# Scaling the attention's latents and shared rotary key on POOL during the input projection, with a round trip through DRAM, in place of DVE at the attention's entry

## The chip, the core and the metric

The kernel runs on one core of a Trainium2 chip. The metric is the device time of one execution in microseconds (us). A core has five engines with queues of their own, each worked off in order: PE (TensorE, matrix products), DVE (VectorE), ACT (ScalarE), POOL (GpSimd) and SP, which here only issues transfers. Sixteen DMA engines move the data. Engines wait for each other through semaphores.

## The reference, cut to what matters

One layer of an encoder on 1024 tokens of width 1024, all in float32. One input projection feeds a convolution branch, a retention branch, a latent attention and a gate; the branches are gated, joined and projected, and the input is added.

```
h = rmsnorm(x, norm_g);  u = h @ w_in            # conv GLU 2*512 | retention q,k,v 3*512 |
                                                 # q-latent 384 | kv-latent 256 | rope key 64 | gate 2048
q  = rmsnorm(q_lat, qa_g)  @ w_uq                # 8 heads x (128 + 64 rotary)
kv = rmsnorm(kv_lat, kva_g) @ w_ukv              # 8 heads x (128 key + 128 value)
k_rope = apply_rope(u_kr, cos, sin)              # one key for all heads
p = softmax((q_nope k_nope + q_rope k_rope) * 192 ** -0.5);  o = p @ v
y = concat(conv, retention, o) * silu(u_gate);   out = rmsnorm(x + y @ w_out, final_g)
```

rmsnorm of a latent is a product of every column (token) with one number, the inverse root of its mean square, and of every row with a weight. The number per token is what the change moves.

## The kernel before, in words

Everything lies transposed: channels on the 128 partitions, tokens along the row. A product in float32 is made of three products of rounded parts (`mm3`, lines 172 to 175): each operand is split into a high part (ACT, a cast) and a low part (DVE, `split_l`, line 66, recorded as line 61).

The input projection is 21 units of 256 columns (`run_unit`), each of four groups of 24 products into one PSUM bank; `run_v` is its form for retention values. Units 0 to 3 make the convolution, 4 to 7 gates, 8 to 10 the latents and the rotary key (`ev_lat`): each half, 128 x 512, is multiplied with the row `rbc`, stored to `l_dram` and squared for the latent's norm. `row_rsqrt` turns the squares into the inverse roots, which go to `lq_dram` and `lk_dram`. Units 11 to 13 make keys, queries and values of the retention, 14 a gate, 15 to 17 the other two heads of the retention, 18 to 20 gates. A retention unit leaves its bank by three DVE products with a table (`ev_rope`, lines 433 to 435); for units 15 and 16 the tables are the two tiles b, loaded at lines 421 and 422 and multiplied with `rbc` on POOL (`trig`). From unit 15 on the projection has only two banks for its groups (`MAIN2`).

Work beside the projection is written as generators in the list `bg`, from which `tick` takes a few steps behind each group: `conv_gen` and `conv_post` (the convolution and its end, with four loads of gates in eight halves, line 373), later `ret_gen` (the retention of one head). Behind unit 14 `drain` empties the list, the pool `cv` on the right side of SBUF is closed, and the pool `rt` of the retention takes its place. Its first tiles are b, the decay index (w, lines 494 and 496), the decay tables Dm, kd and qd made from it, and the pieces w.

The order of the instructions of each engine is not that of the program: the compiler's scheduler lays them out by a simulated timeline, and tiles that reuse memory wait for the last reader of what lay there. Once laid out, each engine's order is fixed.

At the attention's entry (lines 663 to 701) the latents come back: `lat(i, h)` loads half h of latent i from `l_dram`, multiplies it with the broadcast row (`rows`, DVE, line 680), and splits it with the weight into lH (ACT, 681) and lL (DVE). `lat_rows` loads the rows. The rotary key's halves kr are loaded and multiplied with a table (DVE, line 698). The entry's products are `g_k`, `g_r`, `g_kr`, `g_q`, `g_v`; `g_r2` turns the rotary part of q, with four small DMAs and three POOL operations, and Unit.qk (lines 811 to 815) makes the scores.

Of the kernel before, what the change touches and what calls it, by code (L numbers as in the profile page):

```python
# [8 lines left out]
F32 = mybir.dt.float32  # L9
# [4 lines left out]
ADD, SUB, MUL, MAX = ALU.add, ALU.subtract, ALU.mult, ALU.max  # L14

P = 128
S = 1024
D = 1024
KT = D // P
HS = 512  # L20
# [7 lines left out]
QT = 3  # L28
KVT = 2
NG = 16  # L30
EPS = 1e-6
# [23 lines left out]
def body(tc, xT, x, w_in, w_uqn, w_uqr, w_uk, w_uv, w_out, vecs, decay, final_g,  # L55
         t_ret, t_mla, t_idx, t_iota, idm, out):
    nc = tc.nc
    act, dve, pool, pe, sp = nc.scalar, nc.vector, nc.gpsimd, nc.tensor, nc.sync
# [4 lines left out]
    def tt(eng, o, a, b, op):  # L63
        eng.tensor_tensor(o, a, b, op=op)

    def split_l(eng, lo, src, hi, scale=1.0):
        stt(eng, lo, src, scale, hi.bitcast(F32), MUL, SUB)
# [20 lines left out]
    def ps_bg():  # L88
        rr["b"] += 1
        return ps(BG[rr["b"] % len(BG)])  # L90

    def mk(pl, shape, dt=F32, tag=None, bufs=None):
        cnt[0] += 1
        kw = {} if bufs is None else {"bufs": bufs}
        return pl.tile(shape, dt, name=f"{tag}{cnt[0]}", tag=tag, **kw)
# [2 lines left out]
    g_dram = [tc.dram_tile([P, S], F32, name=f"g_dram{i}") for i in range(NG)]  # L98
    y_dram = [tc.dram_tile([P, S], F32, name=f"y_dram{i}") for i in range(NG)]
    l_dram = [tc.dram_tile([P, S], F32, name=f"l_dram{i}") for i in range(QT + KVT + 1)]  # L100

    vec = mk(const, [P, NV], tag="vec")
    rcol = mk(const, [P, KT], tag="rcol")
# [20 lines left out]
    cv = cvx.enter_context(tc.tile_pool(name="cv", bufs=1, side="right"))  # L124
# [90 lines left out]
    bg = []  # L215
# [48 lines left out]
    for k in range(KT):  # L264
# [8 lines left out]
        n = S // 4 if XN[k] == 4 else HS  # L273
# [19 lines left out]
    def row_rsqrt(ss, scale, eps, o, d, col=None):  # L293
        if col is None:
            col = mk(const, [P, KT], tag="rrc", bufs=2)
        c = ps_bg()
        for n in range(KT):
            pe.matmul(c[:, n:n + 1], ss[:, n * P:(n + 1) * P], ones[:, 0:1], start=True, stop=True)  # L298
        dve.tensor_scalar(col, c[:, :KT], scale, eps, op0=MUL, op1=ADD)
        pool.tensor_tensor(col, col, eps_c[:, :KT], op=ALU.pow)  # L300
        pe.transpose(c[:KT, P:2 * P], col, ident)
        row = mk(cv, [P, HS], tag="cb", bufs=2)[:KT, :P]
        act.copy(row, c[:KT, P:2 * P])
        sp.dma_start(d.rearrange("(n p) -> n p", p=P), row)
        if o is not None:
            sp.dma_start(o, d.rearrange("(o s) -> o s", o=1).to_broadcast([P, S]))
# [85 lines left out]
    lss = mk(cv, [P, S], tag="lss")  # L392
    lsk = mk(cv, [P, S], tag="lsk")
# [19 lines left out]
        wn = run_unit(u, wn, ev_lat(2 * (u - 8)), u + 1, 2)  # L413
    lq_dram = tc.dram_tile([S], F32, name="lq_dram")
    lk_dram = tc.dram_tile([S], F32, name="lk_dram")
    for ss, n, d in ((lss, 384.0, lq_dram), (lsk, 256.0, lk_dram)):
        row_rsqrt(ss, 1.0 / n, EPS, None, d)

    def trig(pl, tag):
        c, s_ = mk(pl, [P, S], tag=tag, bufs=2), mk(pl, [P, S], tag=tag, bufs=2)  # L420
# [212 lines left out]
    fin, la, wt, lx = late  # L633
# [26 lines left out]
    def half(i):  # L660
        return slice(i * HS, (i + 1) * HS)

    def row_bc(pl, tag, d, h):
        t = mk(pl, [P, HS], tag=tag)
        sp.dma_start(t, d[half(h)].rearrange("(o s) -> o s", o=1).to_broadcast([P, HS]))
        return t

    krt, rows = [], {}

    def lat_rows(h):  # L670
        rows[1, h] = row_bc(fin, "rb", lk_dram, h)
        rows[0, h] = row_bc(wt, "xh", lq_dram, h)

    def lat(i, h):
        pl, tag, n = LT.pop(0)
        LT.append((pl, tag, n))
        t = mk(pl, [P, HS], tag=tag, bufs=n)
        sp.dma_start(t, l_dram[i][:, half(h)])
        g = vec[:, V_QG + i:V_QG + i + 1]
        tt(dve, t, t, rows[int(i >= QT), h], MUL)  # L680
        act.activation(lH[i][:, half(h)], t, AF.Identity, scale=g)
        split_l(dve, lL[i][:, half(h)], t, lH[i][:, half(h)], g)

    LT = [(lx, "lt", LTB)] * LTB + [(fin, "osb", 2), (fin, "g", 2)] * 2
    lat_rows(0)
    lat(3, 0)
    lat(4, 0)
    W = {("k", 0): lw_k(0)}
    for i in range(QT):
        lat(i, 0)  # L690
# [1 line left out]
    W["q", 0] = lw_q(0)  # L692
    W["v", 0] = lw_v(0)
    for h in range(2):
        t, tk = mk(lx, [P, HS], tag="kr", bufs=2), mk(fin, [P, HS], tag="g" if h else "osb", bufs=2)
        sp.dma_start(t, l_dram[5][:, half(h)])
        sp.dma_start(tk, t_mla[2][:, half(h)])
        tt(dve, t, t, tk, MUL)
        krt.append(t)
    sp.dma_start(cosm, t_mla[0])  # L700
    sp.dma_start(sinm, t_mla[1])
# [51 lines left out]
    def g_r(p, hf):  # L753
        o = up3(W["r", p], 0, QT, hf)
        xr = mk(wt, [P, HS], tag="xr")
        xs = mk(wt, [P, HS], tag="xs")
        act.copy(xr, o)
        for q in range(4):
            s0 = (q ^ 1) * 32
            sp.dma_start(xs[q * 32:(q + 1) * 32], xr[s0:s0 + 32])  # L760
        rst[p, hf] = xr, xs
# [100 lines left out]

    g_k(0, 0)
    g_r(0, 0)
    lat_rows(1)
    lat(3, 1)
    lat(4, 1)
    g_kr()
# [43 lines left out]
    for u in range(NUN):  # L912
# [33 lines left out]
        for i in range(8):  # L946
            cur.qk(i)
            t, j = (i // 2 - 1) % 4, i % 2
# [203 lines left out]
```

## Time and profile before

| what | value |
|---|---|
| median of 3 runs | 1118.09 us (1115.96 to 1120.15) |
| profiled execution, its own time | 1115.07 us |
| span of its trace | 1113.3 us |
| granted PE clock, mean | 0.996 |
| PE busy | 1095.2 us (98%), 5568 instructions |
| DVE / ACT / POOL busy | 724.1 (65%) / 412.6 (37%) / 149.8 us (13%) |

The profile is one execution. "Busy" is time in which the engine had an instruction in work; products of PE overlap, so their durations are longer than the distance from one to the next. The granted clock is the share of full speed (2.4 GHz) that PE's throttle gave. A transfer's "landing" is the time from its issue to its completion.

### The profile page before, as it was taken

How to read it: one execution, taken by the hardware profiler on the slowest of the kernel's cores; microseconds unless marked ns; L12 is line 12 of the kernel's file. 1: busy time of each engine (PE TensorE's matmuls, PEld its weight loads, DVE VectorE, ACT ScalarE, POOL GpSimd, SP SyncE). 2: the span in 40 equal slices, each digit the busy share in tenths (PEclk: the TensorE clock that was granted, in tenths of full speed). 3: DMA queues.
4: the chain of work that ended last, by engine and by line, in shares of the span. 5: the costliest groups of instructions: out<-in, count | busy, mean ns of one | idle time of the engine just before them, and what ended most of it. 6: DMA issues, size and time to landing. Idle time of an engine off the chain costs nothing.

```text
span 1113.3 us, 14293 instructions
## 1 busy us (share of the span) xinstructions
PE 1095.2 (98%) x5568; PEld 919.4 (83%) x5568; DVE 724.1 (65%) x1011; ACT 412.6 (37%) x741; POOL 149.8 (13%) x134
## 2 busy tenths in 40 slices
PE   9999999999999999999899999999999999999997
PEld 7888888888898899888678888888788877888886
DVE  7599999999747695746865565655565572535033
ACT  8211221122144134224654554544554462424022
POOL 0200000214302442020201101100110000001000
PEclk9999999999999999999999999999999999999999
DMA  7221223221262122227211111211210141835013
GB/s 272 95 58 66 86 92 126 85 86 48 97 216 94 49 76 66 96 76 248 79 39 47 56 35 49 62 35 45 63 44 30 57 143 38 308 98 203 25 45 107
DMA packets 45620, 101.33 MB, mean 91 GB/s; under 512 B 5616, under 2 KB 9568, under 8 KB 45552
## 3 DMA queue, kind: packets, MB, share of 16 engines
q1 hardware_dynamic: 45504, 100.35, 27.3%
q8 instruction: 43, 0.70, 0.3%
q14 instruction: 25, 0.20, 0.1%
q0 software_dynamic: 48, 0.08, 0.0%
HBM read 74.14 MB, written 24.17 MB: 88 GB/s over the span
## 4 chain that ended last, share of the span: by engine, by line
PE 93%; DVE 2%; ACT 1%; DMA 1%; issue 1%; SPq 0%; POOLq 0%; POOL 0%; DVEq 0%; ACTq 0%
PE ps L173 24%; PE ps L174 24%; PE ps L175 24%; PE ps L829 5%; PE ps L811 3%; PE ps L815 3%; PE ps L814 3%; PE ps L813 3%; PE ps L812 3%; PE ps L574 1%; PE ps L563 1%; PE ps L298 1%; PE ps L578 1%; PE ps L576 1%; DMA hp<-in_xT_dram 1%
## 5 line engine op out<-in xcount | busy, mean ns | idle before, releaser
L174 PE MATMUL ps<-xL,wh 128*128 128x512 f32 (+1 forms) x612 | 238.1, 390 | 0.1
L175 PE MATMUL ps<-xH,wl 128*128 128x512 f32 (+1 forms) x612 | 237.9, 389 | 0.0
L173 PE MATMUL ps<-xH,wh 128*128 128x512 f32 (+1 forms) x612 | 235.7, 392 | 2.0 <-ACT xH L137 1.5
L61 DVE SCALAR_TENSOR_TENSOR acc<-hp,cwh,acc 128x1024 f32<-128x1024 f32 x120 | 153.0, 1316 | 0.1
L173 PEld LDWEIGHTS ps<-xH,wh 128*128 128x128 f32 x612 | 114.7, 188 | 25.6 <-ACT xH L137 1.7
L174 PEld LDWEIGHTS ps<-xL,wh 128*128 128x128 f32 x612 | 115.0, 188 | 23.8 <-DVE xL L61 0.6
L175 PEld LDWEIGHTS ps<-xH,wl 128*128 128x128 f32 x612 | 114.9, 188 | 23.7 <-issue 0.2
L61 DVE SCALAR_TENSOR_TENSOR PL<-ps,PH 128x512 fp32r<-128x512 f32 x128 | 85.5, 684 | 54.5 <-ACT PH L831 54.3
L831 ACT CAST PH<-ps 128x512 fp32r<-128x512 f32 x128 | 72.8, 588 | 92.6 <-PE ps L829 92.0
L174 PE MATMUL ps<-woL,yh 128*128 128x512 f32 (+1 forms) x264 | 100.9, 386 | 0.0
L175 PE MATMUL ps<-woH,yl 128*128 128x512 f32 (+1 forms) x264 | 100.2, 386 | 0.0
L173 PE MATMUL ps<-woH,yh 128*128 128x512 f32 (+1 forms) x264 | 100.1, 386 | 0.0
L818 DVE TENSOR_REDUCE nm<-ps 128x1 f32<-128x1024 f32 x64 | 78.1, 1220 | 31.8 <-PE ps L815 31.1
L164 ACT CAST wh<-wraw 128x1024 fp32r<-128x1024 f32 x40 | 42.1, 1053 | 126.6 <-PE ps L174 117.0
L820 ACT ACTIVATE P<-ps,nm 128x1024 f32<-128x1024 f32 x64 | 71.6, 1119 | 26.1 <-DVE nm L818 23.7
L829 PE MATMUL ps<-ident,P 128*128 128x128 f32 x512 | 72.7, 273 | 0.0
L829 PEld LDWEIGHTS ps<-ident,P 128*128 128x128 f32 x512 | 61.5, 140 | 12.7 <-DVE PL L61 0.7
L61 DVE SCALAR_TENSOR_TENSOR wl<-wraw,wh 128x1024 fp32r<-128x1024 f32 (+2 forms) x45 | 54.3, 1207 | 7.4 <-ACT wh L164 6.3
L811 PE MATMUL ps<-kH,qH 128*128 128x512 f32 x128 | 55.0, 430 | 3.8 <-DVE qL L61 2.6
L174 PEld LDWEIGHTS ps<-woL,yh 128*128 128x128 f32 x264 | 49.6, 188 | 10.4
L173 PEld LDWEIGHTS ps<-woH,yh 128*128 128x128 f32 x264 | 49.6, 188 | 10.4
L175 PEld LDWEIGHTS ps<-woH,yl 128*128 128x128 f32 x264 | 49.6, 188 | 10.3
(291 smaller groups left out, 1987.0 us busy)
## 6 DMA issues: line engine op xcount, KB each, us to landing
wraw<-in_w_in_dram SPq DMA_DIRECT2D x40, 512.0 KB, 3.5
wor<-in_w_out_dram SPq DMA_DIRECT2D x16, 512.0 KB, 5.0
g_dram<-ga SPq DMA_DIRECT2D x29, 256.0 KB, 2.1
yr<-y_dram SPq DMA_DIRECT2D x18, 256.0 KB, 3.7
g<-g_dram SPq DMA_DIRECT2D x16, 256.0 KB, 3.3
rb<-rs_dram SPq DMA_DIRECT2D x16, 256.0 KB, 3.2
y_dram<-osb SPq DMA_DIRECT2D x16, 256.0 KB
z<-in_x_dram SPq DMA_DIRECT2D x8, 512.0 KB, 3.4
```

Of the source, the lines that this page charges most:

```text
L61: eng.scalar_tensor_tensor(o, a, s, b, op0=op0, op1=op1)
L164: act.copy(hi, t)
L173: pe.matmul(o, sh, mh, start=first, stop=False, skip_group_check=skip)
L174: pe.matmul(o, sh, ml, start=False, stop=False, skip_group_check=skip)
L175: pe.matmul(o, sl, mh, start=False, stop=last, skip_group_check=skip)
L811: pe.matmul(o, qh[:, ts], kh, start=True, stop=False)
L812: pe.matmul(o, qh[:, ts], kl, start=False, stop=False)
L813: pe.matmul(o, ql[:, ts], kh, start=False, stop=False)
L818: dve.tensor_reduce(nm, self.S, axis=AX.X, op=MAX, negate=True)
L820: act.activation(p, self.S, AF.Exp, bias=nm, accum_out=self.rs[:, t:t + 1])
L829: pe.transpose(o[:, c * P:(c + 1) * P], self.p[t][:, (4 * j + c) * P:(4 * j + c + 1) * P], ident)
L831: act.copy(ph, o)
```

## The change

The inverse roots of both latents are also kept as broadcast rows in the pool `cv` (`row_rsqrt` with a target tile, one more 512 KB load each). A new generator, `lat_gen`, goes to the end of `bg`: for each of the twelve halves of five latents and the rotary key it loads the half from `l_dram` into a tile "cb" (two of these, shared with the loads of `conv_post`), multiplies it on POOL with its row, or the rotary key with its table, and stores it to the new tensor `n_dram`. At the entry `lat` loads from `n_dram` and only splits; the row loads, the table loads and twelve DVE products are gone there.

```
     lq_dram = tc.dram_tile([S], F32, name="lq_dram")
     lk_dram = tc.dram_tile([S], F32, name="lk_dram")
-    for ss, n, d in ((lss, 384.0, lq_dram), (lsk, 256.0, lk_dram)):
-        row_rsqrt(ss, 1.0 / n, EPS, None, d)
+    rows = []
+    for ss, n, d, tag in ((lss, 384.0, lq_dram, "lss"), (lsk, 256.0, lk_dram, "lsk")):
+        rows.append(mk(cv, [P, S], tag=tag))
+        row_rsqrt(ss, 1.0 / n, EPS, rows[-1], d)
+
+    def lat_gen():
+        for i in (3, 4, 0, 1, 2, 5):
+            for h in range(2):
+                t = mk(cv, [P, HS], tag="cb", bufs=2)
+                hs = slice(h * HS, (h + 1) * HS)
+                sp.dma_start(t, l_dram[i][:, hs])
+                yield
+                if i < 5:
+                    tt(pool, t, t, rows[int(i >= QT)][:, hs], MUL)
+                else:
+                    k = mk(cv, [P, HS], tag="ca", bufs=4)
+                    sp.dma_start(k, t_mla[2][:, hs])
+                    tt(pool, t, t, k, MUL)
+                sp.dma_start(n_dram[i][:, hs], t)
+                yield
+
+    bg.append(lat_gen())
...
-        sp.dma_start(t, l_dram[i][:, half(h)])
+        sp.dma_start(t, n_dram[i][:, half(h)])
         g = vec[:, V_QG + i:V_QG + i + 1]
-        tt(dve, t, t, rows[int(i >= QT), h], MUL)
         act.activation(lH[i][:, half(h)], t, AF.Identity, scale=g)
         split_l(dve, lL[i][:, half(h)], t, lH[i][:, half(h)], g)
...
-        t, tk = mk(lx, [P, HS], tag="kr", bufs=2), mk(fin, [P, HS], tag="g" if h else "osb", bufs=2)
-        sp.dma_start(t, l_dram[5][:, half(h)])
-        sp.dma_start(tk, t_mla[2][:, half(h)])
-        tt(dve, t, t, tk, MUL)
+        t = mk(lx, [P, HS], tag="kr", bufs=2)
+        sp.dma_start(t, n_dram[5][:, half(h)])
```

The two calls of `lat_rows` and `row_bc` are gone as well. In the changed kernel the lines move: `lat_gen`'s load is line 427 and its store 435, the tables b are loaded at 442 and 443, the decay index at 515 and 517, the bank's evictions stand at 454 to 456.

The scheduler's order changes with it. On SP, at the end of unit 14, the loads of the tables b stood right behind the convolution's last store (y_dram) and the weights (wraw):

```order
L375 DMA y_dram_83<-acc_369 128x1024
L163 DMA wraw_2714<-in_w_in_dram 128x1024
L421 DMA b_2601<-in_t_ret_dram 128x1024
L422 DMA b_2602<-in_t_ret_dram 128x1024
L494 DMA w_2607<-in_t_idx_dram 128x256
L496 DMA w_2609<-in_t_iota_dram 128x256
L212 DMA g_dram_72<-ga_2499 128x512
L212 DMA g_dram_72<-ga_2529 128x512
```

In the changed kernel the same loads on SP stand behind all twelve loads (cb from l_dram) and stores (n_dram) of `lat_gen`, of which these are the last:

```order
L435 DMA n_dram_103<-cb_2542 128x512
L427 DMA cb_2550<-l_dram_98 128x512
L435 DMA n_dram_104<-cb_2546 128x512
L427 DMA cb_2584<-l_dram_101 128x512
L435 DMA n_dram_104<-cb_2550 128x512
L427 DMA cb_2590<-l_dram_101 128x512
L435 DMA n_dram_107<-cb_2584 128x512
L435 DMA n_dram_107<-cb_2590 128x512
L442 DMA b_2663<-in_t_ret_dram 128x1024
L443 DMA b_2664<-in_t_ret_dram 128x1024
L515 DMA w_2669<-in_t_idx_dram 128x256
L517 DMA w_2671<-in_t_iota_dram 128x256
```

The four gate stores (g_dram), which stood behind the tables, now stand between the loads and stores of `lat_gen`.

On PE, in unit 15, the first products of the retention (w with w) stood inside the unit's second group (ps_2724):

```order
L174 MATMUL ps_2724<-xL_122,wh_2487 128x512
L175 MATMUL ps_2724<-xH_114,wl_2488 128x512
L173 MATMUL ps_2728<-w_2697,w_2659 128x256
L174 MATMUL ps_2678<-w_2670,w_2659 128x128
L175 MATMUL ps_2678<-w_2669,w_2660 128x128
L173 MATMUL ps_2678<-w_2669,w_2659 128x256
L174 MATMUL ps_2678<-w_2670,w_2659 128x256
L175 MATMUL ps_2678<-w_2669,w_2660 128x256
```

In the changed kernel PE has them behind the whole second group (ps_2786) and ahead of the third (ps_2850):

```order
L176 MATMUL ps_2786<-xH_125,wl_2532 128x512
L174 MATMUL ps_2740<-w_2731,w_2721 128x128
L544 MATMUL ps_2810<-ident_376,k_1887 128x128 x4
L175 MATMUL ps_2740<-w_2732,w_2721 128x128
L176 MATMUL ps_2740<-w_2731,w_2722 128x128
L174 MATMUL ps_2740<-w_2731,w_2721 128x256
L175 MATMUL ps_2740<-w_2732,w_2721 128x256
L176 MATMUL ps_2740<-w_2731,w_2722 128x256
L174 MATMUL ps_2790<-w_2759,w_2721 128x256
L584 MATMUL ps_2915<-q_1888,k_1887 128x128 x4
L174 MATMUL ps_2834<-w_2825,w_2815 128x256
L174 MATMUL ps_2850<-xH_118,wh_2525 128x512
```

Some 170 products further on, in unit 16, PE's order is again that of before, up to the end. ACT and DVE follow it: the work on Dm, kd and qd stands behind all four gates of unit 14, where it stood between them.

On DVE, at the entry, products with a row or table (line 64) stood among the low parts lL and the gates (xs, xr):

```order
L64 TENSOR_TENSOR kr_4317<-kr_4317,osb_4318 128x512
L61 SCALAR_TENSOR_TENSOR lL_4261<-lt_4273,vec_102,lH_4256 128x512
L64 TENSOR_TENSOR kr_4322<-kr_4322,g_4323 128x512
L61 SCALAR_TENSOR_TENSOR xs_4217<-ps_4192,rbc_128 128x512
L61 SCALAR_TENSOR_TENSOR lL_4257<-lt_4284,vec_102,lH_4252 128x512
L64 TENSOR_TENSOR osb_4371<-osb_4371,rb_4367 128x512
L61 SCALAR_TENSOR_TENSOR xs_4217<-ps_4192,xs_4217 128x512
L61 SCALAR_TENSOR_TENSOR xr_4247<-ps_4222,rbc_128 128x512
L64 TENSOR_TENSOR g_4376<-g_4376,rb_4367 128x512
```

In the changed kernel DVE's entry holds the splits and gates alone:

```order
L61 SCALAR_TENSOR_TENSOR wlr_4354<-wr_4352,whr_4353 128x384
L61 SCALAR_TENSOR_TENSOR xs_4279<-ps_4254,rbc_134 128x512
L61 SCALAR_TENSOR_TENSOR xs_4279<-ps_4254,xs_4279 128x512
L61 SCALAR_TENSOR_TENSOR lL_4319<-lt_4491,vec_108,lH_4314 128x512
L61 SCALAR_TENSOR_TENSOR xr_4309<-ps_4284,rbc_134 128x512
L61 SCALAR_TENSOR_TENSOR lL_4320<-lt_4495,vec_108,lH_4315 128x512
L61 SCALAR_TENSOR_TENSOR wlq_4360<-wr_4358,whq_4359 128x384
```

Twelve rows of line 64 are gone from DVE there, and PE's order at the entry is the same as before.

## Rows read from the trace of the kernel before

**Rows 1.** Busy time by stage, attention's entry: us, PE, PEld, DVE, ACT, POOL, PEclk, DMA share, GB/s
```profile
515.00:530.00 15.00, 14.07 (x60) 11.00 (x59) 14.12 (x24) 7.69 (x13) 0.00 (x0) 1.00 0.99 369
530.00:545.00 15.00, 11.94 (x48) 8.62 (x47) 12.61 (x21) 9.71 (x19) 3.85 (x3) 0.89 0.31 89
```

**Rows 2.** What PE waited for, 505 to 560 us: total us, times, longest
```profile
PE ps L811 <- DVE qL L61: 2.6, 1, 2.6
PE ps L721 <- DVE xr L61: 0.9, 1, 0.9
```

**Rows 3.** Busy time by stage behind the longer wait
```profile
538.00:540.00 2.00, 1.03 (x3) 0.83 (x3) 1.56 (x4) 0.72 (x3) 1.49 (x2) 0.69 0.00 0
540.00:542.00 2.00, 1.94 (x6) 0.97 (x4) 1.90 (x3) 0.44 (x1) 1.92 (x2) 0.50 0.03 8
```

**Rows 4.** Timeline of SP's issues, 322 to 332 us: start, duration, what
```profile
322.58 0.42 SPq L373 DMA_DIRECT2D cb<-g_dram  x1
...
326.84 0.32 SPq L375 DMA_DIRECT2D y_dram<-acc  x1
...
328.35 0.67 SPq L421 DMA_DIRECT2D b<-in_t_ret_dram  x1
...
331.12 0.33 SPq L494 DMA_DIRECT2D w<-in_t_idx_dram  x1
```

**Rows 5.** DVE's groups of instructions, 515 to 540 us: count, busy us, mean ns
```profile
L64 DVE TENSOR_TENSOR lt<-lt,xh 128x512 f32<-128x512 f32 x4 | 2.7, 684 | 0.0
```

**Rows 6.** Timeline of ACT at the entry
```profile
533.85 0.57 ACT L757 COPY xr<-ps 128x512 f32<-128x512 f32 x1
...
542.47 0.62 ACT L769 CAST xh<-xr 128x512 fp32r<-128x512 f32 x1 [2.02 <-POOL xr L64]
```

**Rows 7.** Timeline of PE, unit 15 and the entry
```profile
352.11 0.39 PE L174 MATMUL ps<-xL,wh 128*128 128x512 f32 x1
352.33 0.39 PE L175 MATMUL ps<-xH,wl 128*128 128x512 f32 x1
...
524.07 0.40 PE L175 MATMUL ps<-xH,wl 128*128 128x512 f32 x1
...
544.19 0.39 PE L814 MATMUL ps<-K,QA 128*128 128x512 f32 x1
```

**Rows 8.** DMA issues: count, KB each, median us to landing
```profile
g<-g_dram SPq DMA_DIRECT2D x16, 256.0 KB, 3.3
...
l_dram<-ca SPq DMA_DIRECT2D x12, 256.0 KB, 2.0
...
cb<-g_dram SPq DMA_DIRECT2D x8, 256.0 KB, 4.3
...
wr<-in_w_uv_dram SPq DMA_DIRECT2D x4, 256.0 KB, 2.8
```

**Rows 9.** Tiles g and lss on POOL: duration ns min/median/max, first and last start
```profile
L64 POOL TENSOR_TENSOR g<-g,rb x16: 1280/1286/1687, 574.9 to 946.9; 128x512 f32<-128x512 f32 x16
...
L64 POOL TENSOR_TENSOR lss<-lss,cb x4: 1538/1808/2269, 208.1 to 220.1; 128x512 f32<-128x512 f32 x4
```

**Rows 10.** Timeline of DVE, decay tables and evictions of unit 15's first bank
```profile
336.31 3.52 DVE L507 TENSOR_SCALAR Dm<-w,lg 128x128 f32<-128x128 f32 x4 [4.41 <-DMA w<-in_t_idx_dram]
...
342.41 0.68 DVE L61 SCALAR_TENSOR_TENSOR ga<-ps,ga 128x512 f32<-128x512 f32 x1
343.01 0.48 DVE L510 TENSOR_SCALAR Dm<-Dm 128x128 f32<-128x128 f32 x3
...
352.15 0.69 DVE L433 TENSOR_TENSOR w<-ps,b 128x512 f32<-128x512 f32 x1 [0.62 <-PE ps L175]
...
353.56 0.68 DVE L435 TENSOR_TENSOR w<-ps,b 64x512 f32<-64x512 f32 x1
```

**Rows 11.** Timeline of ACT, exponentials of the decay tables and the first splits
```profile
343.05 0.39 ACT L513 ACTIVATE qd<-qd,lg 128x128 f32<-128x128 f32 x1
...
348.73 1.70 ACT L533 ACTIVATE w<-v,kd 128x256 fp32r<-128x256 f32 x4
```

More of the change, by code (lines that the diff above doesn't have):

```diff
@@ L100, in body @@
     l_dram = [tc.dram_tile([P, S], F32, name=f"l_dram{i}") for i in range(QT + KVT + 1)]
+    n_dram = [tc.dram_tile([P, S], F32, name=f"n_dram{i}") for i in range(QT + KVT + 1)]
     vec = mk(const, [P, NV], tag="vec")
@@ L661, in half @@
         return slice(i * HS, (i + 1) * HS)
[L663 to L672, printed above, removed]
+    krt = []
     def lat(i, h):
@@ L684, in body @@
     LT = [(lx, "lt", LTB)] * LTB + [(fin, "osb", 2), (fin, "g", 2)] * 2
-    lat_rows(0)
     lat(3, 0)
@@ L864, in body @@
     g_r(0, 0)
-    lat_rows(1)
     lat(3, 1)
```

## The prediction

> **What bounds the kernel now.** I read the page first, then the windows by stage, the waits of PE, and the timelines of SP, POOL, DVE and ACT around the two places that the change touches. PE is busy for 98% of the span, so the end moves only with PE's idle time, its clock, or work added to its queue. The attention's entry is one of the few places where PE idles: from 515 to 545 us it is busy 14.07 of 15 us and then 11.94 of 15, while DVE is busy 14.12 of the first 15 and the DMA engines 0.99 [rows 1]. PE waited there 2.6 us for the split of the first q and 0.9 us for a gate's last product, both on DVE [rows 2]; behind the longer wait the granted clock was 0.69 and then 0.50 [rows 3]. So the entry can give back at most 3.5 us of waiting and 1.5 us of slow clock (half of the 1.0 us that PE was busy before 540, half of the 2 us behind it): 5.0 us.
>
> The other place is the end of unit 14, from 320 us on. PE has no idle time there that the change could remove. What matters is which buffers come free when: SP issues the last gate load of the convolution at 322.58, the last store at 326.84, the rotary table b at 328.35 and the decay index at 331.12 [rows 4], and nothing behind them stops PE.
>
> **What is removed.** Twelve DVE products at 0.68 us [rows 5], 8.2 us of DVE time in a stretch in which DVE had 0.9 us free, and six loads of 256 KB (four broadcast rows, two halves of the rotary table). That is more than the 3.5 us of waits. What is late next is the rope of the first q: its copy on ACT at 533.85 starts a chain (four small DMAs, three POOL operations) that reaches ACT again at 542.47 and lets PE begin the rope products at 544.19 [rows 6, 7]. With ACT and DVE free, the copy can run when its products end, near 528; the same 8.6 us then end at 536.6, and two more ACT copies at 538. PE comes there after its last product of unit 20 at 524.07 plus 20.1 us, less the 5.0 above: 539.2. It just fits. I take 4.5 us gained; the bounds are 2 (the rope late by 3 us) and 5.0.
>
> **What is added.** Twelve chains of load, POOL product and store, on two buffers of 512 columns, all through SP's one queue. POOL is nearly idle, so its own time costs nothing. But the loads are tied: a half's load waits until the store two before it has landed, since it writes the same buffer. One turn of a buffer is a load, a product, a store and an issue. A 256 KB load lands after 3.3 us where the DMA engines are quiet, 4.3 where the convolution's stores run, 2.8 for the fastest kind; a 256 KB store after 2.0 [rows 8]. The POOL product of this shape takes 1.29 us in the attention and up to 2.27 beside DVE's work [rows 9]. I take 3.3 + 1.3 + 2.0 + 0.3 = 6.9 us, since after 350 little runs beside it; the bounds are 6.4 and 7.7.
>
> In the trace the same POOL operation is slower where DVE is busy [rows 9]. The Trainium skill (SBUF — State Buffer, section "Who interferes with whom") says that a DVE instruction with two SBUF inputs and a GpSimd instruction that reads SBUF shut each other out for a whole instruction. That speaks against moving products to POOL: by it the first three turns, beside the gates' and weights' splits, cost about 1 us more each, and the sum below would be 3 us larger.
>
> The first load can leave SP behind the last gate load, at 323.0. It lands after 4.3 us, its product ends at 328.6, its store and then the second load leave at about 329 (the convolution's last store is out at 326.84, so that buffer is free). From the second load to the twelfth are five turns: 329 + 34.5 = 363.5. Its product ends 4.6 us later and its store leaves at 368.1. Only then, as SP's order shows, comes the load of table b: 368.4 instead of 328.35 [rows 4]. Bounds: with 2.8 us for loads 363.8; with 7.7 us for a turn 374.
>
> From b's load to the moment at which PE may go on: the index load leaves 1.3 us behind it and in the trace lands 5.2 us after its issue (331.12 to 336.31), behind the same megabyte. From the first decay table operation to the last one 7.2 us pass, 1.2 of them two gate operations (0.68 us each, overlapping a little) that now stand earlier: 6.0 [rows 4, 10]. ACT's exponentials ended at 343.4, beside DVE's last table operation, with one 0.6 us gate operation among them against DVE's two; without these ACT is the later one by 0.5 us. Then ACT and DVE split the first values (0.43 us each, three of them and a DVE split: 1.8) [rows 11], and only behind these stand the three evictions of unit 15's first bank, 2.1 us [rows 10]. Together 6.5 + 6.0 + 0.5 + 1.8 + 2.1 = 16.9; I take 17, with 15 and 19 as bounds (two loads less in the queue; POOL's two table products in the way, as they were before). So the bank is free at 385.4.
>
> When does PE want it? Unit 15 has two banks for its own products. Its first group ended when DVE's eviction began, at 352.15 [rows 10]; in the new order PE runs the second group without retention products between, 24 times the 0.23 us between 352.11 and 352.33 [rows 7], and stands at 357.6. What lies in its queue before the third group is retention work that hangs on the same tables, some 2 us (1 to 3). Dead time: 385.4 - 357.6 - 2 = 25.8. In the kernel before, the bank was free at 354.24 and PE never waited for it: the change eats that slack and then 26 us more.
>
> After it PE starts slowly. At the entry the clock was 0.50 just behind a wait of 2.6 us [rows 2, 3], which cost 1.5; I take 1.5, between 1 and 3, since no row shows a wait as long as this one. The Trainium skill (TensorE: Matmul & The Clock Gate, Part 1) says that the engine's default is throttled and that activity releases it. By that rule a longer wait costs one slow start, not more; the fall to 0.50 agrees, and the sum is the same.
>
> Further on, the queues of PE and DVE stand as before, so what PE lost isn't won back, and I count no second wait. That is the least sure zero: while PE runs its next two groups, some 20 us, DVE has about as much to do, and its cover is gone if one of them is late; then 1 to 3 us more.
>
> **Sum.** +25.8 + 1.5 - 4.5 = +22.8 us. The profiled execution before took 1115.07 us (its span is 1113.3), so 1137.9; the median of the three runs is 3.0 above that execution, which makes 1140.9. I take 1139. Its own bounds: 363.8 + 15 - 357.6 - 3 + 1 - 5.0 = +14 and 374 + 19 - 357.6 - 1 + 3 - 2 = +35, the second with everything late at once, so I stop at +35 and start at +12.
>
> **Rivals.** (1) The background holds: b's load is out early enough and only the entry's gain is left, 2 to 5 us: 1113 to 1116, no change or barely faster. For it: POOL has 15 us of work and is 13% busy, and the loads need nothing new. It decides from b's load leaving by 340 (357.6 - 17): then five turns would have 11 us, 2.2 us a turn, about what the store alone takes [rows 8]. The tied buffers speak against it. 6%. (2) The chain runs but is quick, with 6.4 us a turn and less behind b's load: the +14 above, 1129 to 1132. For it: the DMA engines are quiet after 350; against: each landing in the rows is longer than 2.8 for loads from a working tensor. 20%. (3) POOL's products and DVE's hold each other up and the queue behind the restart is late as well: 7.7 us a turn, +30 to +35, 1146 to 1153. For it: POOL's slow rows; against: DVE has nothing to do for most of the wait. 15%. (4) The change does not do what it says at the entry, because the rope or ACT's copies keep PE waiting: the sum without 4.5 us, 1143 to 1146. 7%. My forecast, 1133 to 1143: 52%.
>
> Faster or slower by more than 0.5% (5.6 us, about what a measurement can tell here): case 1 lies mostly within it, so faster 2%, same 4%; all others are slower, 94%. The range takes in cases 2 to 4: 1128 to 1153.
>
> **What would show it.** In the new trace PE has one wait of 20 us or more, starting near 357 us, put down to DVE or ACT (the split values or the evictions), with a clock near 0.5 behind it; SP issues the load of b near 368; twelve POOL products of about 1.3 us lie between 327 and 368 in pairs some 7 us apart; from unit 20's end to the first rope product pass some 15 us instead of 20.1. Wrong would be: b's load before 350; no wait over 5 us between 340 and 400; or PE still waiting 2.6 us for q at the entry.

## The result and the profile after

| kernel | time, us (median, lowest to highest) | runs |
|---|---|---|
| before | 1117.23 (1115.96 to 1120.15) | 4 |
| changed | 1148.89 (1146.45 to 1151.91) | 4 |

The changed kernel takes 1.0281 times as long, with a 95% interval of 1.0257 to 1.0304. Its profiled execution took 1149.53 us, of which the span is 1147.8 (before: 1113.3), so 34.5 us are to be found between the two traces.

Nearly all of them stand in one place. Busy time by stage, with the columns of [rows 1]:

```profile
340.00:360.00 20.00, 16.34 (x74) 13.18 (x73) 4.94 (x6) 5.28 (x7) 6.01 (x5) 1.00 0.69 209
360.00:380.00 20.00, 0.00 (x0) 0.00 (x0) 0.69 (x1) 0.00 (x0) 6.65 (x6) 0.50 0.54 183
380.00:400.00 20.00, 12.26 (x63) 10.97 (x64) 16.84 (x37) 7.45 (x22) 9.71 (x6) 0.73 0.05 17
```

PE does nothing from 360 to 380, and DVE and ACT almost nothing; only POOL and the DMA engines work. What PE waited for from 340 to 440 us, with the columns of [rows 2] (before, PE waited 0.5 us in this stretch):

```profile
PE ps L174 <- ACT w L554: 31.4, 1, 31.4
PE ps L174 <- DVE w L456: 3.0, 1, 3.0
PE ps L599 <- DVE Sb L61: 1.0, 1, 1.0
```

L554 (ACT) scales the first values of the retention, L456 is the last eviction of a bank, Sb the retention's states. Why L554 was late is read from SP's issues, the counterpart of [rows 4]:

```profile
325.57 0.73 SPq L427 DMA_DIRECT2D cb<-l_dram  x1
...
331.80 0.32 SPq L435 DMA_DIRECT2D n_dram<-cb  x1
332.17 0.43 SPq L427 DMA_DIRECT2D cb<-l_dram  x1
...
370.64 0.32 SPq L427 DMA_DIRECT2D cb<-l_dram  x1
371.21 4.13 SPq L435 DMA_DIRECT2D n_dram<-cb  x2
375.39 0.42 SPq L442 DMA_DIRECT2D b<-in_t_ret_dram  x1
...
376.34 0.43 SPq L515 DMA_DIRECT2D w<-in_t_idx_dram  x1
```

The second load leaves at 332.17, the twelfth at 370.64: five turns of 7.7 us. Table b, which left at 328.35 before, leaves at 375.39. The two kinds of transfer (columns of [rows 8]) and the products on POOL (columns of [rows 9]) fill such a turn:

```profile
cb<-l_dram SPq DMA_DIRECT2D x12, 256.0 KB, 3.4
n_dram<-cb SPq DMA_DIRECT2D x12, 256.0 KB, 2.8
```
```profile
L64 POOL TENSOR_TENSOR cb<-cb,lss x6: 1261/1276/1294, 345.5 to 367.0; 128x512 f32<-128x512 f32 x6
...
L64 POOL TENSOR_TENSOR cb<-cb,lsk x4: 1295/1552/2119, 330.0 to 343.4; 128x512 f32<-128x512 f32 x4
...
L64 POOL TENSOR_TENSOR cb<-cb,ca x2: 1262/1262/1262, 369.9 to 373.7; 128x512 f32<-128x512 f32 x2
```

Behind the last store the decay tables, ACT's scaling and the rotary evictions follow, as in [rows 10, 11]; the timelines of DVE, ACT and PE:

```profile
377.61 0.69 DVE L61 SCALAR_TENSOR_TENSOR w<-ps,w 128x512 fp32r<-128x512 f32 x1 [29.14 <-DMA n_dram<-cb]
...
381.23 3.49 DVE L528 TENSOR_SCALAR Dm<-w,lg 128x128 f32<-128x128 f32 x4 [2.93 <-DMA w<-in_t_idx_dram]
...
390.32 0.68 DVE L456 TENSOR_TENSOR w<-ps,b 64x512 f32<-64x512 f32 x1
```
```profile
387.19 1.69 ACT L554 ACTIVATE w<-v,kd 128x256 fp32r<-128x256 f32 x4
```
```profile
387.74 0.47 PE L174 MATMUL ps<-w,w 128*128 128x128 f32 x1 [31.40 <-ACT w L554]
...
391.51 0.40 PE L174 MATMUL ps<-xH,wh 128*128 128x512 f32 x1
```

The first of these rows shows a second tie to the chain besides SP's order: DVE's split of a retention piece w, which uses no scaled latent, waited for the last store to land. That fits the pool `rt` taking the place of `cv`, where the buffers cb lay.

So PE stands from 356.3 to 387.74, then runs 3.8 us of retention products, and the third projection group begins at 391.51, when its bank has been free for half a microsecond. The clock behind the long wait, and behind the wait of 3.0 us that ended at 417.75 (columns of [rows 3]):

```profile
380.00:390.00 10.00, 2.26 (x11) 2.26 (x12) 8.31 (x24) 6.03 (x19) 4.24 (x2) 0.50 0.09 32
...
418.00:420.00 2.00, 2.00 (x6) 1.56 (x6) 1.97 (x4) 0.00 (x0) 1.06 (x1) 0.54 0.00 0
```

At the attention's entry the change does what it says. PE's waits from 540 to 600 us, and the rope's copy and rounding on ACT (the rows of [rows 2, 6] before):

```profile
PE ps L822 <- DVE QA L61: 1.0, 1, 1.0
PE ps L819 <- DVE qL L61: 0.8, 1, 0.8
PE ps L174 <- DVE kL L61: 0.6, 1, 0.6
PE ps L819 <- DVE vL L61: 0.2, 1, 0.2
```
```profile
567.46 0.59 ACT L765 COPY xr<-ps 128x512 f32<-128x512 f32 x1 [1.65 <-DMA g_dram<-xr]
...
577.19 0.62 ACT L777 CAST xh<-xr 128x512 fp32r<-128x512 f32 x1 [3.12 <-POOL xr L64]
```

The last projection product and the first rope product on PE, as in [rows 7]:

```profile
561.35 0.40 PE L176 MATMUL ps<-xH,wl 128*128 128x512 f32 x1
...
578.67 0.47 PE L822 MATMUL ps<-K,QA 128*128 128x512 f32 x1 [1.03 <-DVE QA L61]
```

The wait for q fell from 2.6 to 0.8 us, and from unit 20's end to the rope pass 17.3 us instead of 20.1. Unit 20 ends at 561.35 and the span 586.5 us later; before these were 524.07 and 589.2. The entry gave back 2.8 us in this pair (37.3 less 34.5). The rest of the account: unit 20 ends 37.3 us later, and the waits above are 31.4 + 3.0 + 1.0 = 35.4; 1.9 are left. In these stand, with opposite signs, the slow clock, an estimate of 3.3 us (the share below 1.00 of the time that PE was busy, 1.6 from 387.74 to 391 and 1.7 from 418 to 422), and 1.2 us of waits that only the kernel before had: 0.7 more at the start and 0.5 at the retention.

### The profile page after: what moved, and what is told of

Same layout as the page of the kernel before. It is cut to its first block, busy times and chain, and to the rows that moved or that the text cites. A ratio compares the mean times of both kernels' runs of the same rounds, so it can differ in the third digit from the quotient of the medians.

```text
span 1147.8 us, 14357 instructions
## 1 busy us (share of the span) xinstructions
PE 1096.6 (96%) x5568; PEld 920.5 (80%) x5568; DVE 718.3 (63%) x999; ACT 412.2 (36%) x741; POOL 165.8 (14%) x146
## 4 chain that ended last, share of the span: by engine, by line
PE 84%; DMA 7%; DVE 3%; issue 1%; POOL 1%; ACT 1%; SPq 1%; POOLq 0%; ACTq 0%; DVEq 0%
PE ps L174 21%; PE ps L175 21%; PE ps L176 21%; PE ps L837 4%; PE ps L819 3%; PE ps L822 3%; PE ps L823 3%; PE ps L821 3%; PE ps L820 3%; DMA cb<-l_dram 2%; DMA n_dram<-cb 1%; POOL cb L64 1%; DMA cb<-g_dram 1%; PE ps L595 1%; PE ps L299 1%
## 5 line engine op out<-in xcount | busy, mean ns | idle before, releaser
L64 POOL TENSOR_TENSOR g<-g,rb 128x512 f32<-128x512 f32 x16 | 20.6, 1291 | 253.5 <-DMA rb<-rs_dram 208.4
```

## The experiments

The first four are against a before of 1117.23 us, the next four 1118.19, the last two 1117.78 and 1117.86.

| kernel | first latent load | b's load | PE's wait for ACT's scaling | PE starts again | time, us | ratio, 95% |
|---|---|---|---|---|---|---|
| changed | 325.57 | 375.39 | 31.4 | 387.74 | 1148.89 | 1.0257 to 1.0304 |
| 1 background alone | 328.30 | 380.08 | 34.1 | 392.60 | 1152.19 | 1.0276 to 1.0355 |
| 2 entry alone | none | 327.36 | none | | 1113.02 | 0.9944 to 0.9982 |
| 3 no product | 323.51 | 364.94 | 19.0 | 377.24 | 1139.64 | 1.0179 to 1.0262 |
| 4 four buffers | 302.36 | 349.42 | 3.7 | 361.56 | 1122.44 | 1.0028 to 1.0065 |
| 5 whole rows, early | 233.02 | 335.42 | none | | 1112.39 | 0.9938 to 0.9974 |
| 6 and tables later | 234.46 | 338.23 | none | | 1111.81 | 0.9930 to 0.9968 |
| 7 products on DVE | 328.00 | 373.98 | 24.7 | 386.27 | 1145.88 | 1.0229 to 1.0281 |
| 8 half the rows | 324.32 | 352.69 | 8.0 | 366.15 | 1127.92 | 1.0071 to 1.0122 |
| 9 decay early | 326.45 | 376.58 | 19.4 + 5.7 | 379.20, 390.26 | 1147.15 | 1.0241 to 1.0302 |
| 10 gate buffers | 233.18 | 334.87 | none | | 1112.92 | 0.9932 to 0.9965 |

The wait depends on when PE gets there as well as on when it may go on. PE stopped at 356.3 us in the changed kernel and at 357.9 to 361.6 in the other profiles with this wait. Most of that is the clock: from 250 to 260 us, with PE busy throughout, it was 1.00 in the changed kernel, but 0.83 in experiments 1, 3, 4 and 8 and 0.66 to 0.69 in 7 and 9 (two of the rows stand at the end). So 1.5 to 5 us of a shorter wait are no gain of the edit; the start of PE is the better measure.

**Experiments 1 and 2: the two halves of the change apart.** One keeps the background and has the entry of before, the other drops the background and reads the unscaled rows.

```diff
 # 1, in lat and for the rotary key
-        sp.dma_start(t, n_dram[i][:, half(h)])
+        sp.dma_start(t, l_dram[i][:, half(h)])
+        tt(dve, t, t, rows[int(i >= QT), h], MUL)
```
```diff
 # 2
-    bg.append(lat_gen())
 ...
-        sp.dma_start(t, n_dram[i][:, half(h)])
+        sp.dma_start(t, l_dram[i][:, half(h)])
```

> The background loads, products and stores as in the changed kernel; the attention's entry as before (loads the unscaled rows, DVE multiplies them by the row scales). Theory (the chain of two-buffer turns costs all of it, the entry only gives back): PE's wait on the first retention bank stays at 31 us (29 to 33), the wait of 2.8 us between the last projection and the first attention product comes back, and the time is 1149 + 3 to 5 = 1152 to 1154 us. Rival A (the new entry itself costs, by loads of the scaled rows that land late): below 1147 us. Rival B (the entry gains nothing): 1147 to 1150 us.

> No background pass; the entry loads the unscaled latents and rotary key and multiplies nothing, so this leaves the scaling by the row scales and by the table out. Theory: no wait at the retention, the whole of the entry's gain shows: before's 1117.2 less 3 to 5 = 1112 to 1114 us. Rival A (the entry is worse for its loads): over 1118 us. Rival B (no gain, another work is late at once): 1116 to 1118 us.

PE's waits of the background alone, at the retention and at the entry:

```profile
PE ps L174 <- ACT w L554: 34.1, 1, 34.1
...
PE ps L832 <- DVE qL L61: 2.6, 1, 2.6
PE ps L742 <- DVE xr L61: 0.9, 1, 0.9
```

The entry's two waits are back to the tenth of a microsecond, and the time is 3.3 us above the changed kernel. The wait is 3 us longer than the 31 expected; b's load left 4.7 us later in this execution, since the chain began 2.7 us later and took 2.0 longer. The entry alone is 4.2 us faster than before. So the two halves add up: the entry is worth 3.3 to 4.2 us, and all of the loss is the background's.

**Experiment 3: the turn without its product.**

```diff
-                    tt(pool, t, t, rows[int(i >= QT)][:, hs], MUL)
 ...
-                    k = mk(cv, [P, HS], tag="ca", bufs=4)
-                    sp.dma_start(k, t_mla[2][:, hs])
-                    tt(pool, t, t, k, MUL)
```

The two loads of the rotary table, which nothing then reads, go with the products.

> The background loads and stores stay, POOL's twelve products are taken out (this leaves the scaling out). Theory (the turn of a buffer is load, product, store in series, 7.7 us as measured): six turns lose some 1.3 to 1.6 us each, so the wait of 31.4 us on the first retention bank becomes 22 to 24 and the time 1139 to 1142 us. Rival A (POOL's products hold DVE or are held by it, and this makes the delay): the wait falls under 12 us, the time under 1130. Rival B (only the extra transfers and the place in SyncE's queue count): no change, 1147 to 1150 us.

SP's issues, the first load to b's:

```profile
323.51 0.73 SPq L427 DMA_DIRECT2D cb<-l_dram  x1
...
364.58 0.32 SPq L433 DMA_DIRECT2D n_dram<-cb  x1
364.94 0.43 SPq L440 DMA_DIRECT2D b<-in_t_ret_dram  x1
```

From the first latent load to b's pass 41.4 us where the changed kernel takes 49.8. The 8.4 us are six turns of 1.4, as much as POOL's mean product in the changed kernel, though the transfers did not stay as they were (loads rose to 4.7 us, stores fell to 2.0). The wait fell by 12.4, more than the 8 expected, because the chain also began 2 us earlier and PE stopped 2 us later. The time lies where the series of load, product and store puts it; both rivals are out.

**Experiment 7: the product on DVE.** Both products of the background with `tt(dve, ...)` in place of `tt(pool, ...)`.

> As the changed kernel, with the twelve background products on VectorE in place of POOL. Theory (turn in series; VectorE's product of this shape takes 0.7 where POOL's takes 1.3 us, and VectorE is idle there): a turn is 0.6 us shorter, the six turns some 3 to 4 us, the wait 27 to 29 us and the time 1144 to 1147 us. Rival A (POOL and VectorE hold each other up): the wait falls below 20 us, under 1138. Rival B (VectorE's own queue, in which the products stand behind evictions and weight splits, holds them): the wait grows to 35 us or more, 1150 to 1156 us.

From first load to b's 46.0 us: 3.8 less, six times 0.64, and DVE's product takes 0.69 where POOL's mean was 1.39. The time is as expected, the wait (24.7) lies under the 27 to 29. PE starts again only 1.5 us earlier, since the first load left 2.4 later; the other 5.2 us of the shorter wait are PE's own lateness (it stopped at 361.6), of which the clock of 0.69 from 250 to 260 us took some 3. POOL and DVE holding each other up does not make the delay. The Trainium skill (SBUF — State Buffer, "Who interferes with whom") says that a DVE instruction with two SBUF inputs contends with a POOL instruction that reads SBUF, for a port pair that it calls an exclusive lock. In the changed kernel the trace agrees: the two of POOL's twelve products that began while DVE split a weight (wl from wraw and wh, both in SBUF, at 329.40 and 343.16 for 1.22 us) took longer than the 1.26 to 1.30 us of the others:

```profile
329.97 1.81 POOL L64 TENSOR_TENSOR cb<-cb,lsk 128x512 f32<-128x512 f32 x1 [25.19 <-DMA cb<-l_dram]
...
343.42 2.12 POOL L64 TENSOR_TENSOR cb<-cb,lsk 128x512 f32<-128x512 f32 x1 [3.98 <-DMA cb<-l_dram]
```

Only these two were held, which is 1.4 us in all, and not the 3 of the prediction's estimate.

**Experiment 8: half the turns.**

```diff
-        for i in (3, 4, 0, 1, 2, 5):
+        for i in (3, 4, 0):
```

> As the changed kernel, but only three of the six rows go through the background (the other three are read unscaled at the entry, so their scaling is left out). Theory (each turn of the two buffers adds about 7.2 to 7.7 us to the wait, linearly): three turns less, 22 to 23 us, so a wait of 8 to 10 us and 1125 to 1128 us. Rival A (a fixed cost, by the first late load or by the place in SyncE's queue): the wait stays over 20 us, over 1138. Rival B (a wait appears only past some length of the chain, other work being late first): no wait at all, 1113 to 1117 us.

```profile
PE ps L174 <- ACT w L554: 8.0, 1, 8.0
PE ps L174 <- DVE w L456: 3.5, 1, 3.5
```

The chain is 21.4 us shorter, 7.1 for each of three turns, and the wait 23.4 shorter (1.8 of it because PE stopped later). The cost goes with the turns, as far as two lengths of the chain can show it. The second wait does not shrink with the first: 3.5 us here, 3.0 in the changed kernel.

**Experiment 4: four buffers.**

```diff
-                t = mk(cv, [P, HS], tag="cb", bufs=2)
+                t = mk(cv, [P, HS], tag="ca", bufs=4)
 ...
-                    k = mk(cv, [P, HS], tag="ca", bufs=4)
+                    k = mk(cv, [P, HS], tag="cb", bufs=2)
```

> The background uses the four buffers ca (free since the rotary units) in place of the two buffers cb; the same loads, products and stores. Theory: twelve halves pass in three turns of four in place of six of two; a turn is at least as long as before (7.7 us) and may be 1 to 2 us longer because four products of 1.3 us follow each other on POOL; the wait of 31 us loses 3 x 7.7 less 3 to 6 = 17 to 20 us, so it is 11 to 15 us and the time 1128 to 1132 us. Rival A (POOL's pace or contention with DVE makes the delay): no shorter wait, 1147 to 1150 us. Rival B (the place of the stores in SyncE's queue makes it): at most 5 us less, 1143 to 1148 us.

The wait is 3.7 us and the time 1122.44: better than expected, and for another reason. SP's issues of this kernel:

```profile
302.36 0.89 SPq L427 DMA_DIRECT2D ca<-l_dram  x2
...
349.42 0.42 SPq L442 DMA_DIRECT2D b<-in_t_ret_dram  x1
```

From the first load to b's pass 47.1 us, hardly less than with two buffers. But the first load leaves 23 us earlier, since the ca buffers are free when the rotary units end, while cb serves the convolution's tail until 325. So this run does not show that fewer turns make the chain shorter (experiment 8 does); it shows what the start is worth.

**Experiments 5 and 6: the same work early, and the tables behind it.** Whole rows in the convolution's four row buffers, ahead of its tail; in 6 also:

```diff
+            T[n] = mk(cv, [P, S + 2 * HALO], tag="hp", bufs=4)[:, :S]
+            sp.dma_start(T[n], l_dram[I[n]])
 ...
-    bg.append(lat_gen())
+    bg.insert(0, lat_gen())
 # 6: behind lat(4, 1) instead of ahead of it
+    sp.dma_start(cosm, t_mla[0])
+    sp.dma_start(sinm, t_mla[1])
```

> The same six rows, scaled by POOL and stored, but as whole rows of 1024 in the four buffers hp (free when the convolution is over), the loads issued at once after the latents' units and ahead of the convolution's tail. Theory (only the late end of the chain costs): the last store is over long before 340 us, no wait of more than 2 us at the retention, the entry's gain remains: 1112 to 1115 us, as the entry alone without any scaling (1113.0). Rival A (POOL's products or the added 6 MB of transfers cost by themselves, by contention with DVE or with the weights' loads): 1117 to 1123 us. Rival B (delayed tail of the convolution makes a new late chain into the retention): a wait of 3 to 10 us there, 1117 to 1125 us.

> As the run with early whole rows, but at the entry the loads of the attention's rotary tables (two of 512 KB) are issued after the first loads of the second half of the latents instead of ahead of them. Theory (with DVE's products gone the entry waits for the landing of its loads, the DMA engines being busy at 0.95 to 1.05 there): the latents land up to 5.7 us earlier, PE's waits of 1 us each at the entry fall, 1 to 3 us less: 1109 to 1113 us. Rival (the conversions on ScalarE and VectorE are what is late): no change against the early whole rows (within 1 us), or 1 to 2 us more if POOL's rotary products now wait for the tables.

In experiment 5, one group of POOL's products, and on SP the first load, the last store and b's load:

```profile
L64 POOL TENSOR_TENSOR hp<-hp,lss x3: 2396/2402/3398, 268.7 to 281.6; 128x1024 f32<-128x1024 f32 x3
```
```profile
233.02 0.32 SPq L427 DMA_DIRECT2D hp<-l_dram  x1
...
288.81 0.32 SPq L442 DMA_DIRECT2D n_dram<-hp  x1
...
335.42 0.66 SPq L451 DMA_DIRECT2D b<-in_t_ret_dram  x1
```

The last store leaves more than 80 us earlier than in the changed kernel, b's load is out at 335.42, and at the retention PE waits 0.5 us, as before. The time is that of the entry alone, so POOL's seven products (five whole rows, the key's two halves) and 6 MB of transfers cost nothing that can be measured: this version takes 0.3 to 0.6% less than the kernel before. The transfers are of 512 KB here, and their medians are 4.2 us for a load and 3.7 for a store, against 3.4 and 2.8 for half as much. The Trainium skill (DMA: Bandwidth & Descriptors, "Anatomy of one DMA") gives a fixed part of about 2 us and a part by bytes, fitted for transfers that GpSimd issues; an estimate by it is 2.6 us for 256 KB and 3.2 for 512. The ratio of 1.23 agrees with the load (1.24, and 1.21 by the 4.1 us of experiment 6), but not with the store, which took 1.32 times as long here and 1.71 times (4.8 us) in experiment 6; the level is too low for all of them.

Experiment 6 does not differ from 5 (PE's waits from 515 to 600 us are 3.6 against 3.4), as its rival had it: the tables' place at the entry is not what is late there.

**Experiment 9: which link ends the wait.**

```diff
+    iote = mk(cv, [P, S + 2 * HALO], tag="hp", bufs=4)[:, :2 * P]...
+    sp.dma_start(iote, t_iota)
+    dve.tensor_scalar(kd[:, 0:4], lg[:, 0:4], iote[:, 1, 1:2], None, op0=MUL)
 ...
+        if h == 0:
+            late_tables()      # Dm and qd
```

> As the changed kernel, but the eight decay factors kd come from their table during the input projection, and the matrices Dm and qd are computed only where the retention first uses them; the twelve turns and the loads of the second rotary tables stay where they are. It asks which link behind the last store ends PE's wait. Theory A (the index tables and what hangs on them, kd and Dm, end it: the wait of 31.4 us ended on the first operand scaled by kd): that wait falls to 22 to 26 us; then the third projection group waits 0 to 4 us for its bank, freed by VectorE's rotary products, and the time is 1141 to 1146 us. Theory B (the second rotary tables end it, as the prediction had it): PE's waits on the two together stay within 1.5 us of 34, whatever name stands at them, and the time is 1147 to 1151 us.

```profile
379.20 0.47 PE L174 MATMUL ps<-w,w 128*128 128x128 f32 x1 [19.43 <-ACT w L557]
...
390.26 0.58 PE L174 MATMUL ps<-w,w 128*128 128x256 f32 x1 [5.67 <-ACT w L557]
390.64 0.68 PE L174 MATMUL ps<-xH,wh 128*128 128x512 f32 x1
```
```profile
378.64 1.71 ACT L557 ACTIVATE w<-v,kd 128x256 fp32r<-128x256 f32 x4 [28.27 <-DMA n_dram<-cb]
```

PE starts its retention products 8.5 us earlier, as theory A has it, stops again for ACT, which now has the tables in front of the next scaling, and reaches the third projection group at 390.64 where the changed kernel was at 391.51. The rotary evictions of its bank end at 390.5. The time is in theory B's range, and its interval (1144.7 to 1151.5) reaches into A's, but neither theory holds as it stands. For B the waits should have stayed near 34 us; they are 25.1, or 28.6 with a wait of 3.5 for the rotary evictions further on. For A the time should have fallen with them. It did not, because PE had come 3.4 us later in this execution and because it ran both pieces at a clock of 0.50, by the same estimate as above 2 us more of slow clock than in the changed kernel. So no single link ends the wait: index tables, rotary tables and the work on both hang behind the same last store and are done within a few microseconds of each other.

With the decay factors ready, ACT's first scaling waited for no table any more but for the landing of the last store, like DVE's split in the changed kernel; that fits its piece w lying where a buffer cb lay. So a place further ahead in SP's queue would bring the tables earlier, but by this run PE would still not start before 379 us as long as the chain ends where it does. No run moves the tables alone. In six kernels the first retention product starts 12.1 to 13.5 us behind b's load (changed: 387.74 against 375.39).

**Experiment 10: the next thing late at the entry.**

```diff
-        gpool[:] = [wt, "xr", 1, wt, "xs", 1]
+        gpool[:] = [fin, "rb", 1, wt, "xh", 1]
```

> As the run with early whole rows, but the last gates of the input projection go through the two buffers rb and xh, which the new entry no longer needs, in place of xr and xs, which the first rope wants. In the changed kernel ACT's copy of the first rope waited 1.65 us for the gate's store from xr, and PE later 1.0 us for the rope's operand. Theory (that store is what is late at the entry once VectorE's products are gone): the copy starts 1 to 2 us earlier after the last projection product, PE's waits there go from 3.4 us to 2.4 or less, and the time is 0.5 to 1.5 us less: 1110.5 to 1112 us. Rival (the splits of k and q on VectorE are late at the same time): the copy moves, PE's waits do not, 1112 to 1113 us. That the median moves by so little may not be told from no change; the waits in the trace decide.

ACT's copy of the first rope, in experiment 5 and here:

```profile
532.61 0.59 ACT L774 COPY xr<-ps 128x512 f32<-128x512 f32 x1 [1.62 <-DMA g_dram<-xr]
```
```profile
529.66 0.58 ACT L774 COPY xr<-ps 128x512 f32<-128x512 f32 x1
```

The wait for the gate's store is gone, and the copy starts 4.5 us after unit 20's end (525.18) instead of 6.1 (526.54). PE's waits from 515 to 600 us are 2.8 against 3.4, and not 2.4 or less: the wait of 0.8 us for q is gone, but one of 1.0 for the rope's operand QA stands there instead. 1112.92 cannot be told from 1112.39. That the store held the copy is shown, a gain is not.

## Why the prediction was right, and where it was off

The mechanism was the forecast one: the two tied buffers hold SP's queue, table b and the index leave 45 to 47 us late, and PE stands once for over 20 us. The time was 10 us above the forecast, inside the range, and above the likeliest case's own band of 1133 to 1143. The range held it only by its upper part, which was drawn for the third rival, whose cause was not at work; that is partly luck. Point by point:

- **First load.** Forecast 323.0, measured 325.57; the second 332.17 instead of 329.
- **The turn, the largest term that was mis-sized.** Forecast 6.9 us, measured 7.7, five times: 4.0 us. I had taken 2.0 for the store, from stores that leave one at a time [rows 8]; in the chain the median is 2.8. Load and product were nearly right (3.4 for 3.3, a mean of 1.4 for 1.3). That the store is slower beside the other buffer's load, the weights and the gates (DMA share 0.54 to 0.76 there) fits, but no run separates it: without the product the stores fell back to 2.0 and the loads rose to 4.7.
- **b's load** left at 375.39 for 368.4: 7.0 late, the two points above.
- **From b's load to the free bank.** Forecast 17, measured 15.6 (391.00). The bank was the wrong milestone, though: PE's queue has retention products first, and these waited for the same tables. I counted them as 2 us done ahead of the end; they began at 387.74. Dead time 31.4 for 25.8: PE stopped 1.3 earlier and started 4.3 later than forecast.
- **The slow clock.** 1.5 forecast for one slow start. The granted clock was 0.50 behind the long wait, which cost an estimated 1.6. The Trainium skill (TensorE: Matmul & The Clock Gate, Part 1) has activity release the throttle, by which a longer wait costs one slow start and not more. The trace agrees for the 31 us. It has a second such start, at 0.54, behind the wait of 3.0 us; these 1.7 us were not in the sum.
- **The second wait**, "the least sure zero", was 4.0 us (3.0 and 1.0). This step failed: DVE's chain of states and evictions was the later one in the next groups. PE stood 1.0 us for the states Sb, DVE then 2.65 for PE's products on them (L599), and the bank's evictions are behind both in DVE's order. It is there in every kernel with the first wait: 3.0 us in experiments 1 and 3, 1.7 in 4, 3.1 in 7, 3.5 in 8 and 9.
- **The entry.** −4.5 forecast; −2.8 in the profiled pair, 3.3 and 4.2 by experiments 1 and 2. The rope's copy ran 6.1 us after unit 20 instead of 4, held 1.65 us by the gate's store from its buffer, a transfer that my chain did not have.

The differences add up: 5.6 (dead time) + 4.0 (second wait) + 1.8 (clock) + 1.7 (entry), less 1.2 (the waits that only the kernel before had), make 11.9, and 34.5 less the forecast 22.8 is 11.7. The number is the one that the third rival gave, turn and late queue both; its cause, POOL and DVE holding each other up, is worth 1.4 us and was not it. The first rival's point of decision, b's load out by 340, was near: with 338.23 there was no wait, with 349.42 one of 3.7.

## What to carry to other kernels

Work that is moved into the background is free only if its buffers and its queue are: before counting it as hidden, write down the chain of one buffer (load, product, store, issue), multiply by the turns, and see what stands behind the last one in the same queue, and what takes over the buffers' memory. The engine that did the product mattered by 0.6 us a turn; where the chain began and how many turns it had mattered by tens. The same work with free buffers, its last store more than 80 us earlier, kept the whole gain.

## What was not expected of the hardware

- A store of 256 KB took 2.0 us (median) in the input projection and in the chain without products, but 2.8 to 3.9 in the chains of experiments 4, 7 and 8 and of the changed kernel, where loads, weights and gates were under way beside it; which of these it is stays open.
- PE's clock fell without any wait. From 250 to 260 us PE was busy throughout, but the granted clock was 1.00 in the kernels before and changed (first row) and in experiment 2, and 0.66 to 0.83 in the nine others (second row, experiment 7: 0.50 from 254 to 260). What PE ran up to there was the same in all of them: 32 products of a single column (L299, in the kernel before L298; ones with lss and lsk). Why the clock fell in one execution and not in the other stays open.

```profile
250.00:260.00 10.00, 10.00 (x56) 8.59 (x57) 9.93 (x12) 0.26 (x1) 6.34 (x2) 1.00 0.40 131
250.00:260.00 10.00, 10.00 (x49) 8.78 (x48) 9.96 (x12) 1.05 (x1) 4.58 (x2) 0.69 0.40 131
```

- Behind a wait of some 3 us the clock was not always the same: 0.54 in the changed kernel (3.0 us), but 1.00 in experiments 1, 7 and 9 (3.0, 3.1 and 3.5 us). Behind the waits of up to 1.0 us at the new entry it stayed at 1.00:

```profile
567.00:582.00 15.00, 12.38 (x57) 9.18 (x56) 8.79 (x13) 7.86 (x16) 3.98 (x3) 1.00 0.20 50
```
